# Turning the samples' probabilities by plain transposes, and conditioning chunks in pairs, in a two-layer decoder step

## The chip, the cores and the metric

The kernel runs on one core of a Trainium2 chip. The core has a matrix engine (TensorE, "PE" in the profile, its weight loads "PEld"), a vector engine (DVE), a scalar engine (ACT), a general engine (POOL) and a queue engine (SP) that issues DMAs; POOL issues DMAs too. TensorE writes only to PSUM, which has eight banks of 512 float32 columns on 128 partitions. The metric is device microseconds of one launch; lower is better.

## The reference

One inference step of a two-layer decoder for a prompt of 512 tokens and for eight samples of eight tokens each. Layer 0 is a gated delta-rule mixer, layer 1 differential attention over shared keys and values, and every norm is modulated by vectors computed from a conditioning input. The two parts that the change touches, cut to their core:

```python
def ada_split(c, w, b, n):                 # conditioning: shift, scale, gate
    return jnp.split(c @ w + b, n, axis=-1)
...
def diff_block(q, k, v, q_pos, k_pos, lam):
    s = jnp.einsum('bqhmd,bkhmd->bhmqk', q, k) * DIFF_DH ** -0.5
    s = jnp.where((k_pos[None, :] <= q_pos[:, None])[None, None, None], s, -jnp.inf)
    p = jax.nn.softmax(s, axis=-1)
    p = p[:, :, 0] - lam * p[:, :, 1]
    return jnp.einsum('bhqk,bkhe->bqhe', p, v)
```

A sample attends to 1024 past tokens (eight pages of 128, found through a page table) and to its own eight. There are eight heads, each with two maps m = 0, 1; a head's probabilities are map 0 minus lambda times map 1. The weight of all conditioning vectors is a 1024 x 8192 matrix, cut into 64 chunks of 128 columns (512 KB each).

## The kernel before

The program is written as generators ("units") that yield an engine, an estimated cost and conditions. A planner (`Weave` for layer 0, its subclass `Second` for layer 1) picks the next unit greedily by its estimates and ranks, and the order it finds is fixed for each engine: each engine's queue runs strictly in that order. A `Room` is a buffer that must be free; `W.leave` gives it back. The large projections have a high rank number, which means low priority: they fill TensorE's time wherever nothing more urgent is ready.

Conditioning. The first 16 chunks are done in an opening stage, 24 chunks (`K.kts`) during layer 0 by `ada_loads` and `ada_units`, and the last 24 in layer 1, in pairs, by `ada_later` and `ada_mod`. In layer 0 one chunk at a time is loaded through SP into the one buffer `araw` (L183), at planned intervals of ADA = 22 us. Its unit then takes the PSUM bank `pa`, which the delta rule's inverse uses as well, and issues eight matmuls (L197) with the conditioning vectors as 32-column weights in four column tiles, a copy of the 128 result columns to `adsb` by ACT (L202), one matmul with the constant `asel` that turns the result (L204), and a DVE add of the bias into `K.mod` (L207).

Layer 0's weights come as pairs of DMAs issued by POOL: a load (L913), a negated rounded copy by ACT (L918), and an accumulating load (L923). POOL's queue is in order, so L923 waits there for ACT, and whatever stands behind it on POOL waits too.

Samples' attention (`Sample2`). Pages of the key and value caches go through PG = 5 buffers `pg`: POOL copies a page's number (L2478), SP loads it and issues the 512 KB DMA (L2483). The order is the keys of samples 0, 1, 2, then values of 0, keys of 3, values of 1, keys of 4, and so on; the values of samples 5, 6 and 7 come last, one after the other.

- `keys`: 16 query columns per head (map 0, map 1) lie in a 32-column group; for each page, eight matmuls with 32-column weights give the scores of all heads, with head h = 2 j + hh in row group j. ACT copies the scores to `p` (name `sp`, 3 buffers, 1088 columns).
- `softmax`: scores with the own tokens, row maximum (DVE), exponential with row sum (ACT), reciprocal, and the matrix `C` [128, 64]. `C` holds for each of the 128 rows (head, map, token) its reciprocal sum, times 1 or minus lambda, in the column of its head and token. One matmul for each of eight pages with `p` as weights and `C` as the moving operand turns, normalizes and combines at once, into [128 keys, 64] (one `px` bank, two such banks); one ACT copy brings all eight to `pTs` (L2564, 2 buffers). A ninth such matmul does the own tokens (`pTn`). `p` and `C` are then given back.
- `values`: bank `po` is first zeroed by a bfloat16 matmul of the zero tile `zb`. Then for each page eight matmuls with eight-column weights from `pTs` accumulate the heads' outputs, eight rows in each group of 32. ACT copies the two blocks to `os` (L2602), two transposes turn them (`W.transpose`, L1932), and DVE copies the result to `oT` (L2609).

Work that fills the time around this: the prompt's attention (`sc`, `pt`, `pv` banks) and the gate projections (called z: `pq` and, late, `pt2`, `sc`, `pv` banks), 24 matmuls of 288 columns for each half tile. After the last page come `samples_end`, the rest of z, and the output projection `out_second`, which needs all of these. `K.mm` shows as L271 in layer 0 and L1927 in layer 1, since helpers record the instructions; so the operands tell the groups apart.

Of the kernel before, what the change touches and what calls it, by code (L numbers as in the profile page):

```python
# [104 lines left out]
def host_consts():  # L105
# [21 lines left out]
    put("amask", np.where(np.arange(8)[None, :] <= r[:, None], 0.0, NEG).astype(np.float32))  # L127
    hq = (p // 16) * 8 + p % 8
    put("comb", (hq[:, None] == np.arange(64)[None, :]).astype(np.float32))
# [46 lines left out]
def ada_loads(K, W, A):  # L176
    at = 0.0
    for n, kt in enumerate(K.kts):
        yield None, 0, at, Room("araw")
        at = W.now + ADA  # L180
        ch = A.araw.tile([128, 8, 128], F32, name="araw")
        W.araw = ch, W.took[0]
        K.nc.sync.dma_start(out=ch[:], in_=K.ada[kt].rearrange("p (k m) -> p k m", m=128))  # L183
        W.load("S", 1.6, "araw", n)


def ada_units(K, W, A):

    nc = K.nc
    for n, kt in enumerate(K.kts):  # L190
        yield "E", None, ("araw", n), Room("pa")
        room, = W.took
        ch, ta = W.araw
        ps = K.pa.tile([128, 512], F32, name="pa")
        for k in range(8):
            j = k % 4
            K.mm(out=ps[32 * j:32 * j + 32, 0:128], lhsT=K.cT[:, k, :], rhs=ch[:, k, :],  # L197
                 start=(k < 4), stop=(k >= 4), tile_position=(0, 32 * j))
# [8 lines left out]
        nc.vector.tensor_scalar(out=K.mod[:, kt, :], in0=ps[:, 128:137], scalar1=K.vec[:, v0:v0 + 1], scalar2=None,  # L207
                                op0=ALU.add)
        W.leave(room)
# [217 lines left out]
class Opening(Weave):  # L427
# [126 lines left out]
    def scale(self):  # L554

        nc = self.K.nc
        yield "A", 0.24, ("r",)
        r = self.K.small.tile([128, 64], F32, name="rsam")
# [228 lines left out]
def phase_a(K, A, ctx, opening):  # L787
# [13 lines left out]

    for name, bufs, roomy in (("u", UB, 1), ("y", YB, 1), ("v", VB, 1), ("z", ZB, 1), ("ss", SSB, 1), ("araw", 1, 1), ("cso", KQS, 1),
                              ("kq", 2, 0), ("kt", 2, 0), ("vr", 4, 0), ("vsm", 2, 0), ("adsb", 1, 0), ("ln", 1, 0),
                              ("gb", 2, 0), ("eg", 4, 0), ("o", 1, 0), ("sm", 2, 0), ("ch", 1, 0), ("st", 2, 0), ("sa", 1, 0)):
# [61 lines left out]
PAD = 0.5  # L866
ADA = 22.0
UB = 4
# [1618 lines left out]
class Sample2:  # L2487
# [5 lines left out]
    def keys(self):  # L2493
# [5 lines left out]
        for hh in range(2):  # L2499
            for m in range(2):  # L2500
                c = hh * 16 + m * 8
                nc.gpsimd.tensor_copy(out=qs[64 * m:64 * m + 64, hh:8:2, c:c + 8],
                                      in_=P.qT[64 * m:64 * m + 64, hh:8:2, SEQ + 8 * b:SEQ + 8 * b + 8])
        yield "Q", 0.15, Room("p")
# [3 lines left out]
        for half in range(2):  # L2508
            for pair in range(2):
# [5 lines left out]
                for n, i in enumerate(ids):  # L2515
                    kp, kr = self.G.tiles["k", i]
                    o = 128 * (2 * pair + n)
                    for hh in range(2):
                        for j in range(4):
                            h = 2 * j + hh  # L2520
                            K.mm(out=S[32 * j:32 * j + 32, o:o + 128], lhsT=qs[:, h, :], rhs=kp[:, h, :],
                                 start=(hh == 0), stop=(hh == 1), tile_position=(0, 32 * j))
# [7 lines left out]
    def softmax(self, qs):  # L2530
# [5 lines left out]
        for hh in range(2):  # L2536
            for j in range(4):
                h = 2 * j + hh
                K.mm(out=pn[32 * j:32 * j + 32, 0:64], lhsT=qs[:, h, :], rhs=P.kT[:, h, SEQ:],
                     start=(hh == 0), stop=(hh == 1), tile_position=(0, 32 * j))  # L2540
# [14 lines left out]
                                op1=ALU.mult)  # L2555
        yield "E", None, Room("px")
        xr, = W.took
# [6 lines left out]
        nc.scalar.copy(out=self.pTs[:], in_=pT[:])  # L2564
        W.leave(xr)
        W.set("pTs", b)
# [4 lines left out]
        K.mm(out=pTn[:, 0:64], lhsT=p[:, 960:1088], rhs=C[:], start=True, stop=True)  # L2571
        W.leave(self.pr, cr)
        yield "D", 0.22
# [4 lines left out]
    def values(self):  # L2578
        W, K, P, b = self.W, self.K, self.W.P, self.b
        nc = K.nc  # L2580
        for pair in range(4):
            ids = [b * NPG + 2 * pair + i for i in range(2)]
            yield "E", None, *[("vpage", i) for i in ids], *((Room("po"),) if pair == 0 else ())
            if pair == 0:
                por, = W.took
                po = K.po.tile([128, 4, 128], F32, name="po")
                K.mm(out=po[:, 0:2], lhsT=P.zb[:], rhs=P.zb[:].unsqueeze(1).to_broadcast([128, 2, 128]), start=True,
                     stop=False)
            for n, i in enumerate(ids):
# [18 lines left out]
        pt = po[:, 2:4].rearrange("p f (j t) -> p f j t", t=32)  # L2608
        nc.vector.tensor_copy(out=P.oT[:, :, b, :], in_=pt[:, :, :, 0:8].rearrange("p f j t -> p (f j) t"))  # L2609
        W.leave(por)  # L2610
# [278 lines left out]
def set_up(W, K, one):  # L2889
# [3 lines left out]
    yield "Q", 1.6, SETUP  # L2893
    for t in P.qs + [P.zb]:
        nc.gpsimd.memset(t[:], 0.0)
# [64 lines left out]
def phase_b(K, ctx, past):  # L2960
# [23 lines left out]
    P.qs = [one.tile([128, 8, 32], F32, name=f"qs{i}") for i in range(2)]  # L2984
    P.zb = one.tile([128, 128], BF16, name="zb")
    P.vn = [one.tile([128, 4, 128], F32, name=f"vn{h}") for h in range(NV)]
# [11 lines left out]
    for name, bufs in (("pp", 3), ("pt", 2), ("px", 2), ("po", 1), ("pg", PG), ("scr", SB), ("ch", CH), ("vch", EV), ("tk", 2), ("raw", 2),  # L2998
                       ("w", 4), ("w2", 3), ("wx", 1), ("qs", 2), ("p", PB), ("pTs", 2), ("os", 1), ("C", 2), ("ls", 2), ("mx", 2),
                       ("pq", 1), ("pt2", 1), ("sc", 2), ("pv", 1), ("pm0", PM[0]), ("pm1", PM[1]), ("pts", 1)):  # L3000
# [207 lines left out]
```

## Time and profile before

| | |
|---|---|
| median of 3 runs | 1168.71 us (1167.85 to 1169.6) |
| the profiled execution | 1167.18 us |
| its span, first to last instruction | 1165.4 us |
| mean granted TensorE clock | 0.996 |

The span is 1.78 us shorter than the same execution's time, and that execution is 1.53 us below the median. Rows of the timeline show the start, the modelled duration, and the instructions merged into the row; durations of neighbouring matmuls overlap, so what a group takes from TensorE is read from start to start. A float32 matmul shows as two records, a transpose as one. In the table by stage, each stretch lists how long each engine was busy in it.

### The profile page before, as it was taken

To read this page: it belongs to the slowest core of one execution; us is meant where nothing else is said; L and a number is where in the kernel's file an instruction comes from. 1 tells how busy PE (TensorE), PEld (TensorE's weight loads), DVE (VectorE), ACT (ScalarE), POOL (GpSimd) and SP (SyncE) were. 2 spreads that over 40 slices of the span, in tenths; PEclk is the share of its full clock that TensorE was granted. 3 is DMA by queue.
4 is the path that set the end of the run, shared out by engine and by line. 5 is a ranking of instruction groups with operands and counts; after the bars stand their busy time and mean duration, and the time that the engine had idled before them with its cause. 6 is when DMAs were issued, how large, how long until landed. Compare 5 with 4: busy or idle time off the path is not lost.

```text
span 1165.4 us, 32715 instructions
## 1 busy us (share of the span) xinstructions
PE 1133.8 (97%) x12771; PEld 1041.2 (89%) x12771; DVE 689.2 (59%) x1739; ACT 688.4 (59%) x1893; POOL 436.4 (37%) x753
## 2 busy tenths in 40 slices
PE   8999999999999999999989999999999999999998
PEld 6899998989989998998989999999997888787998
DVE  4567875776877675867644667474324455543342
ACT  4666867777777777686644243865534556654320
POOL 3343424233333433233223431579923231322341
PEclk9999999999999999999999999999999999999999
DMA  9786666757656674776876888312789899996243
GB/s 367 207 234 157 158 179 147 198 146 201 161 162 157 167 196 123 225 192 175 235 221 158 312 263 302 109 56 84 249 270 341 288 321 319 325 297 217 71 134 114
DMA packets 87643, 239.98 MB, mean 206 GB/s; under 512 B 14450, under 2 KB 28658, under 8 KB 87490
## 3 DMA queue, kind: packets, MB, share of 16 engines
q1 hardware_dynamic: 71938, 181.27, 45.8%
q0 software_dynamic: 15552, 56.63, 22.3%
q8 instruction: 101, 1.65, 0.6%
q14 instruction: 52, 0.43, 0.1%
HBM read 212.02 MB, written 25.84 MB: 204 GB/s over the span
## 4 chain that ended last, share of the span: by engine, by line
PE 78%; ACT 6%; DMA 6%; DVE 3%; issue 3%; POOL 2%; SPq 0%; POOLq 0%; ACTq 0%; DVEq 0%
PE pp L271 23%; PE pp L1927 13%; PE pc L271 7%; PE px L1927 5%; PE pq L1927 5%; PE pt L1927 3%; PE pa L271 3%; PE sc L1927 3%; PE pt L271 3%; PE pt L1932 3%; PE po L1927 3%; DMA wraw<-wall 2%; PE pv L1927 2%; DMA whi<-wall 2%; PE ps L271 2%
## 5 line engine op out<-in xcount | busy, mean ns | idle before, releaser
L271 PE MATMUL pp<-hlo,whi 128*128 128x288 f32 x592 | 170.6, 309 | 0.0
L271 PE MATMUL pp<-hhi,whi 128*128 128x288 f32 x592 | 162.0, 294 | 0.0
L2024 POOL TENSOR_TENSOR wlo<-wraw,whi 128x512 fp32r<-128x512 f32 x82 | 109.7, 1354 | 113.1 <-ACT whi L2018 94.9
L1927 PE MATMUL pp<-hhi,whi 128*128 128x288 f32 x432 | 132.9, 308 | 1.1 <-DVE rst L1830 0.7
L1927 PE MATMUL pp<-hlo,whi 128*128 128x288 f32 x432 | 127.1, 295 | 0.0
L1927 PE MATMUL pp<-hhi,wlo 128*128 128x288 f32 x432 | 125.6, 295 | 0.0
L271 PE MATMUL pp<-hhi,wraw 128*128 128x288 f32 x576 | 124.1, 299 | 0.0
L271 PEld LDWEIGHTS pp<-hlo,whi 128*128 128x128 f32 x592 | 111.5, 188 | 1.8 <-issue 1.4
L271 PEld LDWEIGHTS pp<-hhi,whi 128*128 128x128 f32 x592 | 111.6, 188 | 0.4
L271 PE MATMUL pp<-hhi,wlo 128*128 128x288 f32 x592 | 104.1, 304 | 0.0
L271 PEld LDWEIGHTS pp<-hhi,wraw 128*128 128x128 f32 x576 | 94.3, 189 | 1.0 <-issue 0.4
L1131 DVE SCALAR_TENSOR_TENSOR y<-u,vec,y 128x600 f32<-128x600 f32 x96 | 80.8, 841 | 11.0 <-ACT y L1128 10.4
L1927 PEld LDWEIGHTS pp<-hhi,whi 128*128 128x128 f32 x432 | 81.4, 188 | 5.9 <-issue 4.6
L271 PEld LDWEIGHTS pp<-hhi,wlo 128*128 128x128 f32 x592 | 85.0, 189 | 1.1 <-issue 0.2
L271 PE MATMUL pp<-hlo,wraw 128*128 128x288 f32 x288 | 84.7, 315 | 0.2 <-DVE hlo L1852 0.2
L2478 POOL COPY pg<-ptt 1x1 int32<-1x1 int32 x128 | 27.0, 216 | 149.1 <-PE po L1927 63.4
L1927 PEld LDWEIGHTS pp<-hlo,whi 128*128 128x128 f32 x432 | 81.5, 189 | 0.0
L1927 PEld LDWEIGHTS pp<-hhi,wlo 128*128 128x128 f32 x432 | 80.8, 188 | 0.0
L923 POOL DMA_DIRECT2D wlo<-wall x36 | 32.2, 895 | 119.6 <-ACT wlo L918 75.9
L2018 ACT CAST whi<-wraw 128x1024 fp32r<-128x1024 f32 x47 | 49.0, 1048 | 40.8 <-DMA wraw<-wall 19.7
L1927 PE MATMUL pq<-hhi,whi 128*128 128x288 f32 x184 | 58.9, 320 | 1.0 <-DVE x L2230 1.0
L271 PEld LDWEIGHTS pp<-hlo,wraw 128*128 128x128 f32 x288 | 54.6, 189 | 1.7 <-issue 1.0
(484 smaller groups left out, 3137.5 us busy)
## 6 DMA issues: line engine op xcount, KB each, us to landing
pg<-ck SPq DMA_DIRECT2D x64, 512.0 KB, 5.1
pg<-cv SPq DMA_DIRECT2D x64, 512.0 KB, 5.1
wraw<-wall SPq DMA_DIRECT2D x49, 512.0 KB, 4.4
wraw<-wall POOLq DMA_DIRECT2D x36, 512.0 KB, 5.7
whi<-wall POOLq DMA_DIRECT2D x36, 512.0 KB, 6.0
wlo<-wall POOLq DMA_DIRECT2D x36, 512.0 KB, 5.8
araw<-ada SPq DMA_DIRECT2D x24, 512.0 KB, 4.2
araw<-ada SPq DMA_DIRECT2D x8, 1024.0 KB, 13.7
```

The lines of the kernel that those rows point to most:

```text
L271: return self.K.nc.tensor.matmul(**kw)
L923: K.nc.gpsimd.dma_start(out=lo[:], in_=src, accum_op=ALU.add)
L1131: nc.vector.scalar_tensor_tensor(out=y[:, :YW], in0=u[:, j:j + YW], scalar=cw[j], in1=y[:, :YW], op0=ALU.mult, op1=ALU.add)
L1927: return self.K.nc.tensor.matmul(**kw)
L1932: return self.K.nc.tensor.transpose(**kw)
L2018: nc.scalar.copy(out=hi[:], in_=raw[:])
L2024: (nc.vector if shared else nc.gpsimd).tensor_sub(out=lo[:, q:q + 4], in0=raw[:, q:q + 4], in1=hi[:, q:q + 4].bitcast(F32))
L2478: nc.gpsimd.tensor_copy(out=e, in_=P.ptt[0:1, i:i + 1])
```

## The change

In `ada_loads` and `ada_units`, two chunks go together: two loads at once into two `araw` buffers, planned every 38 us; 16 matmuls into two column ranges of `pa`; one ACT copy of 256 columns, written over the start of the first chunk (the tile `adsb` goes); two turning matmuls; one DVE add for both. Both chunk buffers are given back only after the turning matmuls.

In `Sample2`, the probabilities are turned without `C`: eight plain transposes, in two batches of four, each batch into its own `px` bank and with its own ACT copy of 512 columns. `pTs` has 128 columns per page and one buffer in place of two. The value matmuls take 32-column weights (all 32 rows of a group, both heads' and both maps' rows), so the zeroing matmul and `zb` go, and the first matmul of each row group starts the accumulation. Rows of the other head in a group are computed and not used. At the end, two float32 matmuls with `C` as the moving operand (32 columns each) turn, normalize, combine and choose the rows; they take the place of the two transposes. `C` is kept until then. Heads are laid out as h = j + 4 hh in place of 2 j + hh, in the queries' copies, the scores and the constant `comb`. The own tokens' part (`pTn`) is as before.

A small tile of the opening (`rsam`) moves to another pool.

```diff
 def ada_loads(K, W, A):
...
-        ch = A.araw.tile([128, 8, 128], F32, name="araw")
-        W.araw = ch, W.took[0]
-        K.nc.sync.dma_start(out=ch[:], in_=K.ada[kt].rearrange("p (k m) -> p k m", m=128))
-        W.load("S", 1.6, "araw", n)
+        W.araw = [A.araw.tile([128, 8, 128], F32, name="araw") for _ in range(2)], W.took
+        for kt, ch in zip(K.kts[n:n + 2], W.araw[0]):
+            K.nc.sync.dma_start(out=ch[:], in_=K.ada[kt].rearrange("p (k m) -> p k m", m=128))
+        W.load("S", 3.2, "araw", n)
...
-        for k in range(8):
...
-        W.leave(ta)
-        yield "A", 0.28
-        sb = A.adsb.tile([128, 128], F32, name="adsb")
-        nc.scalar.copy(out=sb[:], in_=ps[:, 0:128])
+        for a, ch in enumerate(chs):
+            for k in range(8):
+                j = k % 4
+                K.mm(out=ps[32 * j:32 * j + 32, 128 * a:128 * a + 128], lhsT=K.cT[:, k, :], rhs=ch[:, k, :],
+                     start=(k < 4), stop=(k >= 4), tile_position=(0, 32 * j))
+        yield "A", 0.4
+        sb = chs[0][:, 0:2, :]
+        nc.scalar.copy(out=sb, in_=ps[:, 0:256].rearrange("p (a m) -> p a m", a=2))
         yield "E", None
-        K.mm(out=ps[:, 128:137], lhsT=sb[:], rhs=K.asel, start=True, stop=True)
+        for a in range(2):
+            K.mm(out=ps[:, 256 + 9 * a:265 + 9 * a], lhsT=sb[:, a, :], rhs=K.asel, start=True, stop=True)
+        W.leave(*tas)
...
-ADA = 22.0
+ADA = 38.0
...
-        pT = K.px.tile([128, 8, 64], F32, name="px")
-        for pg in range(NPG):
-            K.mm(out=pT[:, pg, :], lhsT=p[:, 128 * pg:128 * pg + 128], rhs=C[:], start=True, stop=True)
-        yield "A", act(512), Room("pTs")
-        self.tr, = W.took
-        self.pTs = P.sp.tile([128, 8, 64], F32, name="pTs", bufs=2)
-        nc.scalar.copy(out=self.pTs[:], in_=pT[:])
-        W.leave(xr)
+        self.C, self.cr = C, cr
+        for half in range(2):
+            yield "E", None, Room("px"), *(() if half else (Room("pTs"),))
...
+            pT = K.px.tile([128, 4, 128], F32, name="px")
+            for i in range(4):
+                pg = 4 * half + i
+                W.transpose(out=pT[:, i, :], in_=p[:, 128 * pg:128 * pg + 128], identity=K.ident)
+            yield "A", act(512)
+            if half == 0:
+                self.pTs = P.sp.tile([128, 8, 128], F32, name="pTs", bufs=1)
+            nc.scalar.copy(out=self.pTs[:, 4 * half:4 * half + 4], in_=pT[:])
+            W.leave(xr)
...
-                K.mm(out=po[:, 0:2], lhsT=P.zb[:], rhs=P.zb[:].unsqueeze(1).to_broadcast([128, 2, 128]), start=True,
-                     stop=False)
...
-                        K.mm(out=po[32 * j:32 * j + 8, hf, :], lhsT=self.pTs[:, pg, 8 * h:8 * h + 8], rhs=vp[:, h, :],
-                             start=False, stop=(pg == NPG - 1 and hf == 1), tile_position=(0, 32 * j))
+                        K.mm(out=po[32 * j:32 * j + 32, hf, :], lhsT=self.pTs[:, pg, 32 * j:32 * j + 32], rhs=vp[:, h, :],
+                             start=(pg == hf == 0), stop=(pg == NPG - 1 and hf == 1), tile_position=(0, 32 * j))
...
-            W.transpose(out=po[:, 2 + hf, :], in_=os[:, hf, :], identity=K.ident)
-        W.leave(osr)
+            K.mm(out=po[:, 2, 32 * hf:32 * hf + 32], lhsT=os[:, hf, :], rhs=self.C[:, 32 * hf:32 * hf + 32], start=(hf == 0),
+                 stop=(hf == 1))
+        W.leave(osr, self.cr)
```

More of the change, by code (lines that the diff above doesn't have):

```diff
@@ L177, in ada_loads @@
     at = 0.0
[L178 to L179 removed]
+    for n in range(0, len(K.kts), 2):
+        yield None, 0, at, Room("araw"), Room("araw")
         at = W.now + ADA
[L181 to L184 removed]
+        W.araw = [A.araw.tile([128, 8, 128], F32, name="araw") for _ in range(2)], W.took
+        for kt, ch in zip(K.kts[n:n + 2], W.araw[0]):
+            K.nc.sync.dma_start(out=ch[:], in_=K.ada[kt].rearrange("p (k m) -> p k m", m=128))
+        W.load("S", 3.2, "araw", n)
@@ L187, in ada_units @@
 def ada_units(K, W, A):
     nc = K.nc
-    for n, kt in enumerate(K.kts):
+    for n in range(0, len(K.kts), 2):
+        kt = K.kts[n]
         yield "E", None, ("araw", n), Room("pa")
         room, = W.took
-        ch, ta = W.araw
+        chs, tas = W.araw
         ps = K.pa.tile([128, 512], F32, name="pa")
-        for k in range(8):
-            j = k % 4
-            K.mm(out=ps[32 * j:32 * j + 32, 0:128], lhsT=K.cT[:, k, :], rhs=ch[:, k, :],
-                 start=(k < 4), stop=(k >= 4), tile_position=(0, 32 * j))
-        W.leave(ta)
-        yield "A", 0.28
-        sb = A.adsb.tile([128, 128], F32, name="adsb")
-        nc.scalar.copy(out=sb[:], in_=ps[:, 0:128])
+        for a, ch in enumerate(chs):
[6 more added lines that the diff above has]
+        nc.scalar.copy(out=sb, in_=ps[:, 0:256].rearrange("p (a m) -> p a m", a=2))
@@ L800, in phase_a @@
     W = Weave(K)
-    for name, bufs, roomy in (("u", UB, 1), ("y", YB, 1), ("v", VB, 1), ("z", ZB, 1), ("ss", SSB, 1), ("araw", 1, 1), ("cso", KQS, 1),
-                              ("kq", 2, 0), ("kt", 2, 0), ("vr", 4, 0), ("vsm", 2, 0), ("adsb", 1, 0), ("ln", 1, 0),
+    for name, bufs, roomy in (("u", UB, 1), ("y", YB, 1), ("v", VB, 1), ("z", ZB, 1), ("ss", SSB, 1), ("araw", 2, 1), ("cso", KQS, 1),
+                              ("kq", 2, 0), ("kt", 2, 0), ("vr", 4, 0), ("vsm", 2, 0), ("ln", 1, 0),
                               ("gb", 2, 0), ("eg", 4, 0), ("o", 1, 0), ("sm", 2, 0), ("ch", 1, 0), ("st", 2, 0), ("sa", 1, 0)):
@@ L2571, in softmax @@
         K.mm(out=pTn[:, 0:64], lhsT=p[:, 960:1088], rhs=C[:], start=True, stop=True)
-        W.leave(self.pr, cr)
+        W.leave(self.pr)
         yield "D", 0.22
@@ L2893, in set_up @@
     yield "Q", 1.6, SETUP
-    for t in P.qs + [P.zb]:
+    for t in P.qs:
         nc.gpsimd.memset(t[:], 0.0)
```

27 lines of the change are left out of this document (13 added, 14 removed).

## The prediction

> **What bounds the kernel now.** I read the page's table of engines first, then the shares of the chain of work that ended last, then the busy times in two stretches: layer 0 (40 to 620 us) and the stage of the samples' pages (860 to 1072 us).
>
> ```profile
> PE 1133.8 (97%) x12771; PEld 1041.2 (89%) x12771; DVE 689.2 (59%) x1739; ACT 688.4 (59%) x1893; POOL 436.4 (37%) x753
> ...
> PE 78%; ACT 6%; DMA 6%; DVE 3%; issue 3%; POOL 2%; SPq 0%; POOLq 0%; ACTq 0%; DVEq 0%
> ```
> ```profile
> 40.00:620.00 580.00, 565.14 (x6498) 529.41 (x6497) 402.83 (x1099) 412.53 (x1252) 198.74 (x359) 1.00 0.69 180
> 860.00:1072.00 212.00, 208.58 (x2973) 169.92 (x2973) 97.10 (x256) 114.19 (x335) 57.96 (x158) 1.00 0.89 307
> ```
>
> The columns of the second view are the stretch, its length, then busy time of PE, PEld, DVE, ACT and POOL, the granted clock, the DMA share and GB/s. TensorE is busy 97% of the span, 565 of 580 us and 209 of 212 us in the two stages that change; ACT and DVE have a third to a half of each stage free. Busy alone would not prove a bound, since ends are modelled; but the chain too lies on PE for 78%. So a change is worth what it does to TensorE's time, as long as other TensorE work is ready in the place that is freed. In layer 1 I looked for that work behind the last page, in the chain in order of time:
>
> ```profile
> 1060.45 5.18 DMA pg<-cv
> ...
> 1082.74 3.16 PE pt L1927 x24
> ...
> 1104.99 3.21 PE pq L1927 x24
> ```
>
> The last page lands at 1065.6. From 1082.74 to 1108.20 there are eight half tiles of z and nothing else, 25.5 us; 3.16 us for 24 matmuls is 0.132 us each. In the page stage the DMAs run at 307 GB/s and 0.89 busy, so the pages will hardly end earlier. But what TensorE saves among the pages goes to z, and this pure stretch of z then shrinks by as much. A saving there reaches the end until 25.5 us are used up.
>
> **Conditioning chunks in pairs.** A single chunk's group in layer 0, then the pair's form, which layer 1 already has, with the next instruction's start behind each; then the turning matmuls, single and in a pair:
>
> ```profile
> 248.89 0.29 PE L271 MATMUL pp<-hhi,wraw 128*128 128x288 f32 x1
> 249.11 0.64 PE L271 MATMUL pa<-araw,cT 128*32 128x128 f32 x16
> 249.68 0.40 PE L271 MATMUL pp<-hlo,wraw 128*128 128x288 f32 x1
> 249.93 0.30 PE L271 MATMUL pp<-hhi,wraw 128*128 128x288 f32 x1
> ...
> 646.45 1.08 PE L1927 MATMUL pt<-qT,cT 128*32 128x128 f32 x32
> 647.46 0.40 PE L1927 MATMUL pp<-hhi,whi 128*128 128x288 f32 x1
> 647.70 0.29 PE L1927 MATMUL pp<-hlo,whi 128*128 128x288 f32 x1
> ```
> ```profile
> 510.70 0.28 PE L271 MATMUL pa<-con_ident,adsb 128*128 128x9 f32 x2
> 510.84 0.38 PE L271 MATMUL pp<-hlo,whi 128*128 128x288 f32 x1
> 511.05 0.30 PE L271 MATMUL pp<-hhi,whi 128*128 128x288 f32 x1
> ...
> 648.35 0.51 PE L1927 MATMUL pt<-con_ident,scr 128*128 128x9 f32 x4
> 648.71 0.38 PE L1927 MATMUL pp<-hhi,whi 128*128 128x288 f32 x1
> 648.93 0.29 PE L1927 MATMUL pp<-hlo,whi 128*128 128x288 f32 x1
> ```
>
> Entering the column tiles costs 249.11 - 248.89 - 0.13 = 0.09 us, the group 0.57, leaving 249.93 - 249.68 - 0.13 = 0.12: 0.78 for one chunk, 1.56 for two. The pair takes 0.09 + 1.01 + 0.11 = 1.21, so 0.35 less, and 12 pairs give -4.2 us. The turning matmuls take 0.35 - 0.13 = 0.22 each alone and 0.58 - 0.13 = 0.45 as two: no gain. ACT issues 12 copies for 24 and DVE 12 adds for 24; both lie under TensorE's projections, and I cost that at nothing.
>
> The second load of a pair is new in its place: SP issues 1 MB at once. SP is in order, and today it stands at these loads:
>
> ```profile
> SPq L183 <- PE pa L271: 117.2, 21, 12.0
> ```
>
> That is 117 us in 21 waits, because SP runs ahead of the plan. Behind them wait state loads and outputs, planned for later in any case. With pairs there are 11 such waits, each ending after the turning matmul in place of the chunk's own group, some 2 us later (249.11 to 251.4 here would be the like); nothing on TensorE waits for that as long as the queue stays this far ahead. What the bigger bursts do to weight loads is a rival below.
>
> **The samples, each of eight.** The zeroing and the value group; the product with C; four transposes in one bank; the two closing transposes; a score group, whose weights have 32 columns:
>
> ```profile
> 909.82 0.28 PE L1927 MATMUL po<-zb 128*128 128x256 bf16 x1
> 910.03 1.06 PE L1927 MATMUL po<-pg,pTs 128*8 128x128 f32 x32
> 911.02 2.00 PE L1927 MATMUL px<-C,sp 128*128 128x64 f32 x16
> ...
> 943.96 2.00 PE L1927 MATMUL px<-C,sp 128*128 128x64 f32 x16
> 945.80 0.89 PE L1927 MATMUL pv<-vn,pts 128*128 128x128 f32 x6
> ...
> 885.88 0.65 PE L1932 MATMUL pt<-con_ident,vch 128*128 128x128 f32 x4
> 886.29 0.38 PE L1927 MATMUL pq<-hhi,whi 128*128 128x288 f32 x1
> 886.50 0.30 PE L1927 MATMUL pq<-hlo,whi 128*128 128x288 f32 x1
> ...
> 887.17 0.38 PE L1932 MATMUL po<-con_ident,os 128*128 128x128 f32 x2
> 887.38 0.33 PE L1927 MATMUL px<-C,sp 128*128 128x64 f32 x2
> ...
> 892.12 1.08 PE L1927 MATMUL px<-pg,qs 128*32 128x128 f32 x32
> 893.13 0.44 PE L1932 MATMUL pt<-con_ident,pm 128*128 128x128 f32 x2
> ```
>
> - Eight products with C take 945.80 - 943.96 = 1.84 us. Four transposes take 0.41, and 0.08 more where projections follow; two batches are 0.82 to 0.98. Saved: 0.86 to 1.02, I take 0.90, times eight: -7.2 us.
> - The zeroing matmul takes 0.21, of which 0.09 for entering the column tiles stays: -0.12, times eight -1.0 us.
> - A value group of 32 records takes 911.02 - 910.03 = 0.99 with 8-column weights, a score group 1.01 with 32. Four groups in each sample: +0.08, times eight +0.6 us.
> - The two closing transposes take 0.21. Two float32 matmuls of 32 columns lie between two of 9 columns (0.36, above) and two of 64 (0.46, a quarter of 1.84); nearest to the middle, 0.41: +0.20, times eight +1.6 us.
>
> Together -6.0 us, with ends of -6.0 - 1.0 - 0.4 and -6.0 + 0.3 + 0.4.
>
> ```profile
> L1927 PEld LDWEIGHTS po<-pg,pTs x1024: 85/90/90, 875.0 to 1069.7; 128*8 128x8 f32 x171
> ...
> L2564 ACT COPY pTs<-px x8: 585/592/610, 863.1 to 1040.5; 128x512 f32<-128x512 f32 x8
> ...
> L1927 PEld LDWEIGHTS px<-pg,qs x1024: 106/110/110, 813.9 to 1026.0; 128*32 128x32 f32 x171
> ```
>
> ACT gets eight more copies of 0.59, 4.7 us in a stage where it has 212 - 114 = 98 us free. Its queue is in order, so the prompt's exponentials behind each come 0.59 later, and z covers TensorE meanwhile; without that cover it would be 4.7 us.
>
> The single `pTs` is a new wait: the next sample's transposes start only after the last value matmul of this one. The handoff is 0.41 of transposes, two copies of 0.59, and hops, about 2 us by these rows. Between values of samples 0 to 5 lie eight key pages, which hide it. At 5 to 6 and 6 to 7 nothing lies between, so the samples may end up to 4 us later, at about 1076; z covers that, with 25.5 us. `C` has two buffers and is kept longer, which holds back a softmax two samples ahead; the key pages in between hide this also.
>
> The weights' columns are where the Trainium skill speaks against the change. Rows: 110 ns for a 32-column load against 90 ns for eight, while 32 records of either take 1.01 against 0.99 us. The page "TensorE: Matmul & The Clock Gate" (section "LDWEIGHTS (loading the stationary operand)") has a load's time grow with its columns, P/1.2 ns, which for 24 more columns is an estimate of 20 ns; its section "The mechanism" has loads overlap running matmuls only where the row group differs, and here all use every row. By that rule 1024 x 20 ns would be laid open, and the sum would be some 20 us worse. The trace agrees with the 20 ns and not with their being laid open, since the score groups have the same row groups.
>
> **The sum.** -4.2 - 6.0 = -10.2 us of TensorE time. How much reaches the end I bound by the two readings above: 78% (the chain's share) to 97% (the busy share), -8.0 to -9.9; I take the middle, -8.9. The profiled execution would go from 1167.18 to 1158.3; the runs' median lies 1.53 above that execution, so I forecast 1159.8.
>
> **The rivals.**
>
> 1. *Layer 0 gives nothing back.* The delta rule's chain from group to group might set layer 0's pace, with chunks only filling holes. For it: 580 - 565 = 15 us of idle there, so TensorE does wait now and then. Against: 15 us in 580 is little. Then only the samples' part counts, -6.0 x 0.875 = -5.3: 1163.4.
>
> 2. *New order, no change.* The planner makes a new order from its estimates, and waits that its old order missed may take back the gain. For it: 31.6 us of idle in the span are all that an order can win or lose easily, and a third of that is 10 us. Against: the new pieces have durations that the old ones showed. 1168.7, within 0.2%.
>
> 3. *Slower: pairs of loads hold up layer 0's weights.* One such place today, in the chain, on SP, on POOL, and among TensorE's waits:
>
> ```profile
> 247.97 7.78 DMA whi<-wall
> ...
> 249.81 0.33 SPq L183 DMA_DIRECT2D araw<-ada  x1
> ...
> 257.13 0.88 POOL L923 DMA_DIRECT2D wlo<-wall  x1 [6.49 <-ACT wlo L918]
> ...
> PE ps L271 <- POOL wm L1802: 1.0, 1, 1.0
> ```
>
> A weight load needs 7.78 us with a chunk's load issued into it, ACT's copy comes late, POOL stands 6.49 us at L923 with the mask product (`wm`) behind it, and TensorE waits 1.0 us. A second 512 KB on top costs 0.524 MB / 307 GB/s = 1.7 us of transfer. If each of 12 bursts hits and nothing covers it: 20.5 us, so -10.2 + 20.5 = +10.3, or 1179. It decides from 10.2 / 1.7 = 6 hits out of 12. Against: only one of 24 loads shows such a wait now.
>
> 4. *Slower: wider weight loads are laid open.* 1024 loads x 20 ns = 20.5 us, in the page stage: also +10.3, 1179. It decides from half of the loads. Against: the score groups' 1.01 us.
>
> **How the numbers follow.** Forecast 0.60, rival 1 0.14, rival 2 0.11, rival 3 0.10, rival 4 0.05. The smallest difference that a measurement of this kernel tells from no change is about 0.2%, 2.3 us. Faster: 0.60 + 0.14 = 0.74. Same: 0.11. Slower: 0.15. The range's low end is the full sum with the better ends, -4.2 - 7.4 = -11.6, and with half of the 9 us that a luckier order could win from the idle time of the two stages (18 us, a half of it): about 1152. The high end takes in rivals 1 and 2 and the near part of 3 (up to seven hits): 1171. Left out are most of 3 and 4 and a little below. Within the forecast alone: 1156 to 1163.
>
> **What would show it.** Right: in layer 0, 12 groups of x32 with about 1.0 us to the next start, no copy into `adsb`; in layer 1, transposes of `sp` in fours at 0.41 us, value groups of 32 at 1.01, no `zb`; TensorE's busy time in all about 10 us lower; the span from the last page to the end of z shorter by some 6 us, and the start of layer 1 earlier by some 3 to 4. Wrong: value groups at 1.6 us (rival 4); longer landings of `whi` and POOL waits at L923's place with TensorE idle behind them (3); layer 0 ending where it ended (1); busy time down but idle time up by as much (2). A start of the value group of samples 6 and 7 that is more than 4 us behind the group before it would show that the single `pTs` was priced too low.

## The result and the profile after

| | before | after |
|---|---|---|
| median of 5 runs of each on one chip | 1168.71 us (1164.15 to 1172.65) | 1175.13 us (1172.63 to 1179.25) |
| ratio | | 1.0058, 95% interval 1.0032 to 1.0085 |
| the profiled execution | 1167.18 us | 1179.25 us |
| its span | 1165.4 us | 1177.1 us |
| mean granted TensorE clock | 0.996 | 0.992 |

The changed kernel is slower, where 1159.8 and a range of 1152 to 1171 were forecast. Its profiled execution is the slowest of its five, 4.1 us above their median, so its rows show a little more of the loss than a usual run has. What is said of single places and of layer 0's length below comes from one profiled execution of each kernel; ratios come from all runs. The engines and the chain's shares, from its page:

```profile
PE 1135.5 (96%) x12753; PEld 1047.4 (89%) x12753; DVE 685.9 (58%) x1727; ACT 689.9 (59%) x1889; POOL 437.2 (37%) x752
...
PE 71%; DMA 10%; ACT 6%; issue 6%; DVE 4%; POOL 2%; SPq 0%; POOLq 0%; ACTq 0%; DVEq 0%
```

TensorE's busy time did not fall by 10 us, and the chain has 7 points less of PE and 4 more of DMA. The place is found with the first projection of layer 1, from the timelines of before and of after:

```profile
641.58 0.30 PE L1927 MATMUL pp<-hhi,whi 128*128 128x288 f32 x1
```
```profile
659.44 0.30 PE L1930 MATMUL pp<-hhi,whi 128*128 128x288 f32 x1
```

Layer 1 then takes 1165.4 - 641.6 = 523.8 us before and 1177.1 - 659.4 = 517.7 after: 6.1 less, as forecast. Layer 0 takes 17.8 us more. (Lines have moved by three: L921 is the negation, L916 and L926 are the weight loads, L274 the matmuls.)

Busy times of layer 0, before and then after (stretch, length, PE, PEld, DVE, ACT, POOL, clock, DMA share, GB/s), each with the filler matmuls that the planner puts where it plans idle time:

```profile
40.00:641.40 601.40, 586.54 (x6661) 550.74 (x6660) 413.84 (x1124) 421.29 (x1270) 204.72 (x364) 1.00 0.69 179
```
```profile
L292 PE MATMUL pp<-cT,con_ident 128*128 128x224 bf16 x24 | 2.8, 259 | 2.0 <-DVE v L695 1.0 <-DVE z L1104 1.0
```
```profile
40.00:659.40 619.40, 593.67 (x6694) 560.63 (x6693) 408.37 (x1110) 418.09 (x1256) 204.11 (x364) 0.99 0.67 175
```
```profile
L295 PE MATMUL pp<-cT,con_ident 128*128 128x224 bf16 x62 | 6.8, 260 | 1.5 <-DVE v L698 1.0 <-DVE z L1107 0.5
```

Idle time of TensorE went from 601.40 - 586.54 = 14.9 us to 25.7, which is 10.8 of the 17.8. Busy time rose by 7.1 although the pairs were to take 4.2 out (that figure is the forecast's; a pair's group does take 1.01 us, as from 320.99 to 322.00): fillers give 6.8 - 2.8 = 4.0, and the rest is the clock, below.

Who TensorE and ACT wait for in layer 0 (total us, times, longest), before and after:

```profile
ACT wlo L918 <- DMA whi<-wall: 11.7, 10, 2.4
ACT wraw L918 <- DMA wraw<-wall: 7.9, 3, 3.3
...
PE pa L271 <- ACT V L1670: 2.9, 2, 2.3
PE pa L271 <- ACT WF L1657: 2.8, 3, 1.4
```
```profile
ACT wlo L921 <- DMA whi<-wall: 28.6, 13, 5.0
ACT wraw L921 <- DMA wraw<-wall: 12.7, 7, 4.1
...
PE pa L274 <- ACT V L1648: 7.6, 4, 4.7
PE pa L274 <- ACT WF L1660: 4.2, 4, 2.5
```

ACT stands at its negations for weight loads that have not landed: 41.3 us in 20 waits, 19.6 in 13 before. ACT works in the planned order, and behind the negations stand the copies `V` and `WF` of the delta rule's inverse, for which TensorE then waits. (`V` is copied in several places of the inverse, and the two `V` rows are not the same place: L1648 of after is L1645 of before.) For a weight load itself TensorE waits 0.9 us in after. One such place, from the timeline of after:

```profile
598.16 0.85 POOL L926 DMA_DIRECT2D wraw<-wall  x1 [10.20 <-ACT wraw L921]
598.70 0.86 POOL L916 DMA_DIRECT2D whi<-wall  x1
...
609.41 1.06 ACT L921 ACTIVATE wlo<-whi 128x1024 fp32r<-128x1024 f32 x1 [4.96 <-DMA whi<-wall]
610.88 0.76 ACT L1648 ACTIVATE V<-pa 32x256 f32<-32x256 f32 x2
...
611.69 0.26 PE L274 MATMUL pa<-WC,V 32*32 32x32 f32 x2 [4.67 <-ACT V L1648]
```

POOL, held up for 10.20 us, issues two weight transfers half a microsecond apart; `whi` lands 10.7 us after its issue, ACT stands 4.96 us, and TensorE 4.67. No conditioning chunk is under way here, but SP issues five other transfers of 288 KB between 597.53 and 599.38, so the late landing can't be laid on the two weight loads alone. At 323 us two chunks are under way:

```profile
322.14 1.94 SPq L183 DMA_DIRECT2D araw<-ada  x2
...
323.00 0.87 POOL L916 DMA_DIRECT2D whi<-wall  x1
...
331.69 1.06 ACT L921 ACTIVATE wlo<-whi 128x1024 fp32r<-128x1024 f32 x1 [2.45 <-DMA whi<-wall]
...
334.59 1.48 PE L274 MATMUL pa<-XA,ckq 64*64 64x64 f32 x16 [2.46 <-ACT WF L1660]
```

Here `whi` needs 8.68 us, ACT stands 2.45, and TensorE 2.46. What follows such a stop, in stretches of 5 us (stretch, length, PE busy, clock, DMA share, GB/s), and the clock of the three stretches of 60 us that are not at 1.00 (the last row is the one such stretch of before):

```profile
330.00:335.00 5.00, 2.54 (x24) 1.00 0.13 19
335.00:340.00 5.00, 5.00 (x36) 0.52 0.69 127
340.00:345.00 5.00, 5.00 (x23) 0.50 0.21 75
345.00:350.00 5.00, 4.89 (x38) 0.95 0.47 58
```
```profile
110.00:170.00 60.00, 55.83 (x637) 0.97 0.60 153
...
290.00:350.00 60.00, 57.44 (x677) 0.91 0.59 149
...
590.00:650.00 60.00, 55.01 (x647) 0.97 0.69 192
```
```profile
410.00:470.00 60.00, 58.48 (x717) 0.97 0.62 157
```

A stop of 2.46 us is followed by ten microseconds at half clock, which lose five more. In the three stretches the clock loses (0.03 + 0.09 + 0.03) x 60 = 9.0 us; before, the one stretch loses 1.8 us. The clock is given to two decimals, so these are good to about a microsecond. So the account of layer 0 is: idle +10.8, clock +7.2, fillers +4.0, pairs -4.2, together +17.8.

The samples' part is as it was priced. From the timeline of after: a value group, four transposes of `sp`, the closing matmuls, each read to the next start:

```profile
1074.62 1.08 PE L1930 MATMUL po<-pg,pTs 128*32 128x128 f32 x32
1075.63 0.66 PE L1935 MATMUL px<-con_ident,sp 128*128 128x128 f32 x4
1076.12 0.49 PE L1935 MATMUL pt<-con_ident,pm 128*128 128x128 f32 x3
...
1077.24 0.53 PE L1930 MATMUL po<-C,os 128*128 128x32 f32 x4
1077.61 0.64 PE L1935 MATMUL px<-con_ident,sp 128*128 128x128 f32 x4
```

1.01 us for a value group with 32-column weights, 0.49 for four transposes, 0.37 for the closing pair.

### The profile page after: what moved, and what is told of

The parts are those of the page before. It is cut to its first block, busy times and chain, and to the rows that moved or that the text cites. A ratio compares the mean times of both kernels' runs of the same rounds, so it can differ in the third digit from the quotient of the medians.

```text
span 1177.1 us, 32699 instructions
## 1 busy us (share of the span) xinstructions
PE 1135.5 (96%) x12753; PEld 1047.4 (89%) x12753; DVE 685.9 (58%) x1727; ACT 689.9 (59%) x1889; POOL 437.2 (37%) x752
## 4 chain that ended last, share of the span: by engine, by line
PE 71%; DMA 10%; ACT 6%; issue 6%; DVE 4%; POOL 2%; SPq 0%; POOLq 0%; ACTq 0%; DVEq 0%
PE pp L274 18%; PE pp L1930 14%; PE pc L274 6%; PE pq L1930 6%; PE px L1930 4%; DMA whi<-wall 4%; PE sc L1930 3%; PE po L1930 3%; PE pt L1930 3%; PE pt L1935 3%; PE pa L274 2%; PE pv L1930 2%; PE pt L274 2%; DMA araw<-ada 1%; PE ps L274 1%
## 5 line engine op out<-in xcount | busy, mean ns | idle before, releaser
L274 PE MATMUL pp<-hlo,whi 128*128 128x288 f32 x592 | 173.7, 314 | 0.0
L274 PE MATMUL pp<-hhi,whi 128*128 128x288 f32 x592 | 163.4, 297 | 0.0
L1930 PE MATMUL pp<-hlo,whi 128*128 128x288 f32 x432 | 127.3, 296 | 0.0
L274 PE MATMUL pp<-hhi,wraw 128*128 128x288 f32 x576 | 123.7, 301 | 0.0
L274 PEld LDWEIGHTS pp<-hlo,whi 128*128 128x128 f32 x592 | 112.9, 191 | 1.4 <-issue 0.6
L274 PEld LDWEIGHTS pp<-hhi,whi 128*128 128x128 f32 x592 | 112.8, 191 | 0.5
L274 PE MATMUL pp<-hhi,wlo 128*128 128x288 f32 x592 | 102.4, 302 | 0.9 <-DMA wlo<-wall 0.9
L274 PEld LDWEIGHTS pp<-hhi,wraw 128*128 128x128 f32 x576 | 95.3, 191 | 0.6
L1134 DVE SCALAR_TENSOR_TENSOR y<-u,vec,y 128x600 f32<-128x600 f32 x96 | 84.5, 881 | 15.3 <-ACT y L1131 14.6
L274 PEld LDWEIGHTS pp<-hhi,wlo 128*128 128x128 f32 x592 | 84.7, 189 | 2.2 <-DMA wlo<-wall 1.1
L274 PE MATMUL pp<-hlo,wraw 128*128 128x288 f32 x288 | 84.2, 314 | 0.0
L926 POOL DMA_DIRECT2D wlo<-wall x36 | 32.3, 898 | 115.2 <-ACT wlo L921 62.0
L2021 ACT CAST whi<-wraw 128x1024 fp32r<-128x1024 f32 x47 | 49.0, 1047 | 37.5 <-DMA wraw<-wall 17.9
L1930 PE MATMUL pq<-hhi,whi 128*128 128x288 f32 x192 | 61.9, 322 | 1.6 <-DVE x L2233 1.0
L1930 PE MATMUL pq<-hlo,whi 128*128 128x288 f32 x192 | 56.7, 295 | 0.0
```

The costliest lines, as they stand in the source:

```text
L274: return self.K.nc.tensor.matmul(**kw)
L926: K.nc.gpsimd.dma_start(out=lo[:], in_=src, accum_op=ALU.add)
L1134: nc.vector.scalar_tensor_tensor(out=y[:, :YW], in0=u[:, j:j + YW], scalar=cw[j], in1=y[:, :YW], op0=ALU.mult, op1=ALU.add)
L1930: return self.K.nc.tensor.matmul(**kw)
L2021: nc.scalar.copy(out=hi[:], in_=raw[:])
```

## The experiments

Theories about layer 0. T: bursts of 1 MB hold up the weight loads. R: any other order of the same work loses, since the order of before is an unusually good one; the planner makes a new order whenever a planned time changes. ACT: whatever makes weight loads land late relative to ACT's queue, the loss comes from ACT's stand at the negations. Each ratio is to runs of the kernel before on the same chip, so the medians of different rows do not compare directly. "Layer 1 at" is the start of the first projection of layer 1 in the profiled execution, "ACT waits" the sum of the two rows of the negations (L921 in after, L918 in before) in layer 0, also of that one execution. "Layer 0 by ratio" is an estimate from all runs: what the ratio makes of 1168.7 us, plus the 6.1 us that samples_only saves where the samples' part is in, so how much longer than before's layer 0 it is. It carries the ratio's interval, some 2 to 5 us to either side.

| run | ratio to before, 95% interval | median, us | layer 1 at, us | ACT waits, us | layer 0 by ratio, us |
|---|---|---|---|---|---|
| before | 1 | 1168.71 | 641.6 | 19.6 | 0 |
| after | 1.0058 (1.0032 to 1.0085) | 1175.13 | 659.4 | 41.3 | 12.9 |
| samples_only | 0.9948 (0.9920 to 0.9975) | 1161.23 | 641.9 | 17.7 | |
| pairs_only | 1.0112 (1.0081 to 1.0142) | 1180.96 | 657.2 | 43.0 | 13.1 |
| stagger_pairs | 0.9986 (0.9967 to 1.0005) | 1165.96 | 642.0 | 14.3 | 4.5 |
| before_ada23 | 1.0056 (1.0037 to 1.0076) | 1174.61 | 651.4 | 23.1 | 6.5 |
| after_noload | 0.9981 (0.9957 to 1.0004) | 1164.47 | 645.3 | 34.2 | 3.9 |
| before_noload | 0.9963 (0.9940 to 0.9985) | 1162.50 | 635.1 | 15.6 | -4.3 |
| before_burst | 1.0034 (1.0017 to 1.0050) | 1170.98 | 645.6 | 23.2 | 4.0 |
| after_ada34 | 1.0008 (0.9990 to 1.0027) | 1166.77 | 642.3 | 17.7 | 7.0 |
| after_freeneg | 0.9905 (0.9866 to 0.9944) | 1154.41 | 633.7 | 0 | -5.0 |
| before_freeneg | 0.9958 (0.9935 to 0.9980) | 1161.82 | 636.3 | 0 | -4.9 |
| ada34_late25 | 0.9918 (0.9888 to 0.9947) | 1156.46 | 637.5 | 11.8 | -3.5 |
| after_late16 | 0.9944 (0.9925 to 0.9963) | 1159.76 | 640.7 | 11.9 | -0.4 |
| before_late16 | 1.0003 (0.9987 to 1.0019) | 1166.30 | 639.0 | 8.4 | 0.4 |
| after_ada40 | 0.9980 (0.9960 to 1.0001) | 1163.84 | 645.6 | 21.0 | 3.8 |

**Each part alone.** samples_only is the changed kernel with the old `ada_loads`, `ada_units`, `adsb` and ADA = 22; pairs_only is the kernel before with the new ones and ADA = 38.

> Only the samples' part of the change; layer 0 as before. All theories of the slowdown place it in layer 0, so: layer 0 ends at 641 us as before (640 to 643), the rest of the span is 517 to 519 us for 524, and the time is about 6 us below the kernel before: ratio 0.995 (0.993 to 0.997). If the samples' part costs something that the changed kernel's order only hides, the ratio is 1.0 or more.

> Only the conditioning chunks in pairs; layer 1 as before. All theories: layer 0 ends late, at 650 to 660 us, layer 1 keeps 524 us; ratio 1.009 to 1.014, the changed kernel's 1.0058 plus the 0.005 that the samples' part gives.

samples_only keeps layer 0 where it was and saves its 6 us; pairs_only has all of the loss. By the ratios the parts add up: 13.1 - 6.1 = 7.0 us, against the 6.8 of the whole.

**Pairs planned apart, and a change of nothing but one planned time.** stagger_pairs is the whole change with the two loads of a pair as separate planned steps, 19 us apart:

```diff
+    for n, kt in enumerate(K.kts):
+        yield None, 0, at, Room("araw")
+        at = W.now + ADA / 2
...
-        yield "E", None, ("araw", n), Room("pa")
+        yield "E", None, ("araw", n), ("araw", n + 1), Room("pa")
```

> The whole change, but the chunks of a pair are loaded one by one, 19 us apart; the matmul group is still a pair. Theory of bursts (1 MB at once delays a weight load, ACT stands at its negation, the inverse's copies behind it are late, TensorE idles): ACT's waits for weight loads fall from 41 us to the 20 us of before, layer 0 ends at 638 to 645, ratio 0.988 to 0.995. Theory of order (any other order of layer 0 is some 10 us worse than the one before): layer 0 ends at 650 to 660, ratio 1.002 to 1.012. Theory of the pair's group (a longer hold of its bank): the same as order.

before_ada23 is the kernel before with one number changed:

```diff
-ADA = 22.0
+ADA = 23.0
```

> The kernel before with the chunks' interval at 23 us in place of 22: same work, single loads, another planned order in layer 0. Theory of order: layer 0 ends 5 to 15 us later, ratio 1.004 to 1.013. Theory of bursts: within 3 us of before, ratio 0.998 to 1.003.

The first brought layer 0 back to 642.0 in its profiled execution, the fastest of its twelve, and to some 4.5 us behind before's by the ratio. Yet the loads were not apart on the chip: SP runs ahead of the plan and issued them 0 to 3 us apart (38.96 and 40.21, 68.83 and 70.45, 448.48 and 450.31 us). So it can't test bursts in the way it was meant to. That most of the loss went with the bursts still there speaks against them as the whole cause; it speaks as well against R as it was put, that any other order loses some 10 us. The ratio of 0.9986 lies in neither theory's range. The second lost 9.8 us of layer 0 (6.5 by the ratio) with single chunks and nothing else changed: an order alone can do it. Of the 9.8 us, 4.2 are fillers, 63 in place of 24, which the planner added by itself, and 4.4 are idle.

**The transfers taken away, and bursts put into the old order.** In all three the order on TensorE, ACT, DVE and POOL is that of the kernel they come from. after_noload and before_noload issue one chunk's transfer and use it for all, so they leave out 23 of 24 chunks. before_burst loads two chunks into one double tile and works on them singly (the copy goes over the start of a chunk, as in the changed kernel):

```diff
+        if n % 2 == 0:
+            A.two = A.araw.tile([128, 2, 8, 128], F32, name="araw")
+            for a, k2 in enumerate(K.kts[n:n + 2]):
+                K.nc.sync.dma_start(out=A.two[:, a], in_=K.ada[k2].rearrange("p (k m) -> p k m", m=128))
```

> The changed kernel with the order of TensorE, ACT, DVE and POOL as it is, but without the conditioning chunks' transfers in layer 0 beyond the first: one chunk is loaded once and every pair's matmuls read it twice (left out: 23 of the 24 transfers of 512 KB, so all conditioning vectors of layer 0's part come from one chunk). Theory T (bursts of 1 MB hold up the weight loads): without transfers nothing holds them up, ACT's waits for weight DMAs in layer 0 fall from 28.6 + 12.7 us to under 12, layer 1 starts at 637 to 645 us instead of 659.4, the time is 1152 to 1162. Theory R (any other order of the same work loses, the transfers have no part in it): layer 1 still starts at 653 to 660, the time is 1168 to 1176.

> The same for the kernel before: its order, but the first chunk is loaded once and read by all 24 groups (left out: 23 of 24 transfers). It gives what 23 single transfers cost in the order of before. Theory T and theory R alike: single loads cost little there, 0 to 4 us, so 1163 to 1169 and a start of layer 1 at 638 to 642. If it gains more than 6 us, the transfers cost much in the order of before too, and its order is not a lucky one.

> The kernel before with TensorE, ACT, DVE and POOL in the same order, and the 24 conditioning chunks of layer 0 loaded two at a time into one double buffer; the chunks are still worked on singly, at the same places. Theory T: the bursts alone cost what the changed kernel lost, layer 1 starts at 650 to 660 instead of 641.6, the time is 1176 to 1185, ratio 1.007 to 1.015. Theory R: with the order of before kept, layer 1 starts at 640 to 645, the ratio is 0.998 to 1.003.

Neither theory has it right. Without transfers layer 0 of the changed kernel is 14.2 us shorter (659.4 to 645.3), that of before 6.5 (641.6 to 635.1). By the ratios it is about 9 and 4; of before, 0 to 4 us were expected. But the changed kernel's order still ends its layer 0 10.2 us later than the other with no transfers in either, where its pairs should have made it 4.2 earlier (by the ratios 8.2 later). And bursts in the old order cost 4.0 us (0.34%), where T asked for 8 or more. The landing of `whi` in layer 0, from issue, shows the same two parts (last number: median us; before, after, before_noload, after_noload):

```profile
whi<-wall POOLq DMA_DIRECT2D x34, 512.0 KB, 5.9
```
```profile
whi<-wall POOLq DMA_DIRECT2D x34, 512.0 KB, 6.5
```
```profile
whi<-wall POOLq DMA_DIRECT2D x34, 512.0 KB, 5.5
```
```profile
whi<-wall POOLq DMA_DIRECT2D x34, 512.0 KB, 6.1
```

The chunks add 0.4 us to a landing in either order, and the order adds 0.6 with or without chunks. The Trainium skill ("DMA: Bandwidth & Descriptors", section "Issuing engines are not separate DMA queues") has transfers of all issuing engines interleave on the same sixteen DMA engines; the 0.4 us that SP's chunks cost POOL's loads agree with it.

**The negations freed of their wait.** The order and every transfer stay; ACT's negation reads a constant tile in place of the loaded weights, so these kernels leave out the rounding correction of layer 0's weights:

```diff
-        negative(K, *W.sets[j][:2])
+        lo = W.sets[j][1]
+        K.nc.scalar.activation(out=lo[:], in_=K.ident.unsqueeze(1).to_broadcast([128, 8, 128]), func=AF.Copy, scale=-1.0)
```

> The changed kernel, same order on every engine and all transfers, but ACT's 52 negations in layer 0 read a constant tile (the identity, broadcast) in place of the weights just loaded, so ACT never stands at a negation for a weight load (left out: the rounding correction of layer 0's weights, which becomes another number; the accumulating load still runs). Theory ACT (what costs time in the changed kernel is that ACT, in order, stands 41 us at negations for weight loads that land late, with the inverse's copies behind): layer 1 starts at 636 to 646 us instead of 659.4, ratio to the kernel before 0.985 to 0.998. Rival (TensorE itself waits for the late weights or for other things in this order): layer 1 still starts at 652 or later, ratio above 1.002.

> The same in the kernel before, where ACT stands 19.6 us at negations for weight loads. Theory ACT: a small gain, layer 1 starts at 635 to 640 instead of 641.6, ratio 0.994 to 0.999, so that most of the distance to the changed kernel's layer 0 is gone. Rival: no change, 640 to 643, and the distance stays.

This settles it. Layer 0 of the changed kernel ends 25.7 us earlier (at 633.7, earlier than the expected 636 to 646), that of before 5.3 (by the ratios the kernels gain 17.9 and 4.9). The distance of 17.8 us between them turns into -2.6, and by the ratios 12.9 turns into -0.1. The loss needs ACT's stand: with it gone, nothing of it is left. The stretches of after_freeneg that stood at 0.97, 0.91 and 0.97 in the changed kernel:

```profile
110.00:170.00 60.00, 59.00 (x690) 1.00 0.67 170
...
290.00:350.00 60.00, 59.12 (x715) 1.00 0.60 154
...
590.00:650.00 60.00, 59.68 (x512) 1.00 0.69 216
```

and its whole layer 0, that of before_freeneg, and who TensorE and POOL wait for in after_freeneg:

```profile
40.00:633.60 593.60, 584.14 (x6694) 553.19 (x6693) 406.79 (x1110) 417.58 (x1256) 206.18 (x364) 1.00 0.69 182
```
```profile
40.00:636.30 596.30, 585.86 (x6664) 550.09 (x6664) 414.07 (x1125) 421.65 (x1270) 204.56 (x364) 1.00 0.69 181
```
```profile
PE pc L274 <- ACT wv L1424: 2.7, 7, 0.6
PE pc L274 <- DVE S L1414: 1.2, 5, 0.3
...
PE pa L274 <- ACT WF L1661: 0.7, 1, 0.7
```
```profile
POOL wlo L926 <- ACT wlo L944: 61.2, 19, 6.1
POOL wraw L926 <- ACT wraw L944: 49.4, 10, 11.7
```

Idle time is 593.60 - 584.14 = 9.5 us in place of 25.7, and the 9.0 us of lost clock are back: 16.2 + 9.0 = 25.2 of the 25.7. The same 62 fillers are in it: their busy time stays, and the distance goes all the same. POOL still waits 110.6 us for ACT at its accumulating loads, 121.4 in the changed kernel, and the median `whi` still takes 6.1 us to land. Both are nearly as they were, so neither POOL's hold-up nor the late landing cost the time by itself; what did was ACT, standing there with the inverse's copies behind it.

**Other orders of the whole change.** The planner takes a weight load to be usable 0.6 us after its planned transfer ends, and ranks the negations ahead of almost everything, so each is put at the first planned moment. The next two tell the planner a later landing for first weight loads (ada34_late25 2.5 us, with ADA = 34; after_late16 1.6 us, as shown); with the third and fourth, only ADA differs from the changed kernel (34 and 40); the last has the later landing and the old single chunks.

```diff
-                        self.done[name] = t + (SPARE if "page" in str(name[0]) else LATE), None
+                        self.done[name] = t + (SPARE if "page" in str(name[0]) else 1.6 if name[0] == "hi" else LATE), None
```

> The whole change with pairs planned every 34 us, and the planner told that a first weight load lands 2.5 us after its transfer's end instead of 0.6, so that it places ACT's negations later; no instruction is added or left out. The planner puts layer 0 at 594.1 us with 2.7 us of planned idle (changed kernel: 596.3 with 6.5; kernel before: 598.0 with 2.5). Theory ACT: ACT's waits for weight loads in layer 0 fall under 10 us, layer 1 starts at 634 to 642, 1152 to 1160, ratio 0.987 to 0.995. Rival (orders are a draw that neither the plan nor ACT's waits foretell): 640 to 660, ratio 0.995 to 1.01.

> The whole change with pairs every 38 us, and the planner told 1.6 us in place of 0.6 for a first weight load. It puts layer 0 at 597.2 us with 6.7 us of planned idle. Theory ACT: ACT's waits for weight loads in layer 0 fall from 41 to 15 to 25 us, layer 1 starts at 640 to 650, ratio 0.993 to 1.000. Rival: ACT's waits fall but layer 1 starts at 650 to 660 again, ratio 1.001 to 1.008.

> The changed kernel with its pairs planned every 34 us in place of 38: the same instructions, pairs and bursts in another order; the planner puts layer 0 at 598.0 us against 596.3. Theory T: the bursts hit as before, layer 1 starts at 654 to 662, 1172 to 1179. Theory R: a new draw, with layer 1's start anywhere from 640 to 660, 1157 to 1177; a start under 648 speaks for R.

> The whole change with pairs planned every 40 us in place of 38, with the planner's old landing figure of 0.6 us: one more order of the same instructions, planned at 597.8 us. If ACT's waits for weight loads decide an order's time: the more of them beyond the kernel before's 19.6 us, the later layer 1, by about 0.5 to 1 us for each; under 25 us of waits it starts at 638 to 648, over 35 us at 650 to 662. If orders scatter for another reason, a start over 650 with waits under 25 us, or under 645 with waits over 35 us.

> The kernel before with the planner's figure for the landing of a first weight load at 1.6 us in place of 0.6, and nothing else: single chunks every 22 us, another order. The planner puts layer 0 at 602.3 us with 5.9 us of planned idle (kernel before: 598.0 with 2.5). If the figure by itself shortens layer 0, whatever the chunks: ACT's waits for weight loads fall from 19.6 to under 12 us, layer 1 starts at 634 to 640, ratio 0.991 to 0.997. If it only repairs what the pairs' order had wrong: the waits fall, but the plan is 4 us longer, layer 1 starts at 640 to 647, ratio 0.998 to 1.004.

The expectations of the ACT theory came true for the times and, but for two waits, for the waits: 11.8 us in ada34_late25 is above the 10 that was set, 11.9 in after_late16 below its range. Told 1.6 us, the plan of the changed kernel becomes 0.9 us longer on paper and 13 us shorter on the chip (a ratio of 0.9944 for 1.0058). ACT waits of 11.9 us leave the chunks and their bursts as they are. ADA = 34 and 40, with the old landing figure, lose less: 0.7 and 4.0 us behind before's layer 0 in the profiled executions, 7.0 and 3.8 by the ratios, where the order for 38 loses 12.9. So the order for 38 was a bad draw, and none of the three is a good one. In before, which has few long waits, the landing figure takes the waits to 8.4 us and brings 2.6 us of layer 0 in the profiled execution, but nothing by the ratio, so its start fits the first reading set down for it and its ratio the second. So the figure repaired one order and gained nothing in the other. The wait sum foretells an order's layer 0 only roughly: after_ada34 has 17.7 us of waits and is 7.0 behind by the ratio, and before_ada23 has only 23.1 and starts layer 1 at 651.4. It has a stand of 5.0 us among them:

```profile
ACT wlo L918 <- DMA whi<-wall: 18.1, 10, 5.0
```

But TensorE waits only 1.5 us for `V` and `WF` in that run. So ACT's stand is shown as the cause in the changed kernel's order, and not in before_ada23's; why that one loses stays open. The best of the kernels that leave nothing out is ada34_late25, the whole change with another order: 0.9918, ahead of both kernels. Its interval overlaps that of samples_only, so a gain over that is not shown.

## Why the prediction was wrong

- *The samples, -6.0 us: right.* Layer 1 is 6.1 us shorter in the changed kernel, and samples_only has 0.9948 of 1167, that is -6.1. The value group (1.01), the transposes (0.41 to 0.49 forecast, 0.49 in the place shown) and the closing pair (0.41 forecast, 0.37) were sized from neighbouring rows and came out. The single `pTs` laid nothing open that shows in the sum. The 20 ns of a wider weight load did not show either: 32 records take 1.01 us as the score groups' do, so rival 4 is out, and the rule on weight loads of the same row group (the Trainium skill, "TensorE: Matmul & The Clock Gate", section "The mechanism") does not price this kernel's float32 groups.
- *The pairs, -4.2 us of TensorE work: the group's size is right, the gain at the end is not shown.* A pair's group takes the 1.01 us that layer 1 shows. With the stands gone layer 0 is 2.6 us shorter than before's in one execution each, less than the -3.7 that the forecast's share would be; by the ratios it is 0.1 us shorter, within noise.
- *"How much reaches the end I bound by the two readings above: 78% to 97%": this is the step that failed.* It took layer 0's order, and with it its idle time and clock, as given: what a new order does to the waits stood at nothing in the sum. Of the -10.2 us, the samples' -6.1 came; layer 0 gave +17.8 in the profiled execution, some 13 by the ratios (6.8 slower in all, with 6.1 saved).
- *What the profile of before held and I did not read.* I read the waits of SP, POOL and TensorE, not those of ACT. The 19.6 us of ACT at its negations stood there. I read in them now that negations are planned on the brink of their loads, so that a new order can push any of them over.
- *Rival 3 had the right place and the wrong price.* Late `whi`, ACT behind it, TensorE idle: that is what came. But it was priced at 1.7 us of transfer for each burst, with a chance of 0.10 because one load in 24 showed it. Bursts in the old order cost 4.0 us, not the 20.5 of twelve hits; of the 17.8, the order has 10.2 with no transfers in either kernel. And it looked for the harm at POOL's wait and the mask product behind it; the copies of the inverse behind ACT were hit.
- *Rival 2 had the right cause and the wrong size.* "A third of the idle" was its measure of what an order can lose. An order is not bounded by the idle that is there: it made 10.8 us of new idle, and the clock added 7.2 that no busy or idle row of before shows.

What stays open: which planned times put the 38 us order's negations so close to their loads, what before_ada23's order loses its time to, and how the 14.2 us of after's transfers divide between bursts and bytes, since single loads were not tried in that order.

## What to carry to other kernels

Where a planner fixes the order of in-order queues, a small change of one planned time is a new draw for the whole stage: measure the part in several orders, or with the order held, before its time is credited to the edit. Read the waits of every in-order engine that stands between a DMA and the bounding engine, even an engine that is 59% busy; where its waiting instruction is planned at the first moment a load may land, plan it later. A planner's figure for a load's landing is one such lever: a later one took 13 us off the changed kernel, and nothing off the kernel before.

## What was not expected of the hardware

A short stop of TensorE can cost three times its length: 2.46 us of idle were followed by clocks of 0.52 and 0.50 over ten microseconds with TensorE busy throughout. That the stop brought the slow clock is read from their order in time, and from after_freeneg, where both are gone; no run changed one stop alone. The Trainium skill ("TensorE: Matmul & The Clock Gate", section "What's actually happening") gives a half-rate clock after at least one idle window of about 3.4 us and the full rate after at least one busy window of the same length. The half rate agrees, and a return of some 10 us is within an "at least one". The stop was shorter than that window, and there the measurement decides. Not every stop does this: the one of 4.67 us at 611.69 shows 0.67 for five microseconds and 0.99 in the next:

```profile
605.00:610.00 5.00, 2.03 (x16) 1.00 0.65 220
610.00:615.00 5.00, 3.31 (x57) 0.67 0.42 60
615.00:620.00 5.00, 5.00 (x51) 0.99 1.03 330
```
